# Four blocks of the output product's first token tile placed among the last pair's heads, with one PSUM layout for attention and output product

## The chip, the cores and the metric

The kernel runs on one core of a Trainium2 chip. The metric is the device time of one execution in microseconds (us). Each version is executed several times, and the median counts. The core's engines are TensorE (PE, whose weight loads are listed apart as PEld), VectorE (DVE), ScalarE (ACT), GpSimd (POOL) and SyncE (SP, which here issues nearly all DMAs). Each works through a queue of its own, in order; semaphores tie the queues together.

## What is computed

A trunk of two layers over 1024 tokens of width 1024, in fp32. Layer 0 has attention, layer 1 a recurrent block, and each is followed by a dense SwiGLU network. Only the end of attention and the output product behind it are touched here:

```python
def attention_mixer(h, w_in, rel_bias, w_out):
    ...
    out_a = chunked_relpos_attention(qa, ka, va, rel_bias)
    out_b = stick_breaking_attention(qs, ks, vs)
    return jnp.concatenate([out_a, out_b], axis=-1) @ w_out

def reference(x, ...):
    for layer in range(DEPTH):
        h = rmsnorm(x, norm_mix_pre[layer])
        m = attention_mixer(...) if layer % 2 == 0 else recurrent_mixer(...)
        x = x + rmsnorm(m, norm_mix_post[layer])
        h = rmsnorm(x, norm_ffn_pre[layer])
        x = x + rmsnorm(swiglu(h, ...), norm_ffn_post[layer])
    return x
```

There are 8 heads of the chunked softmax kind (`out_a`) and 8 of the stick-breaking kind (`out_b`), each 64 wide.

## The kernel before

**Heads in pairs.** `attention` (line 265) treats the 16 heads as 8 pairs of 128 columns; `p < 4` are softmax pairs, `p >= 4` stick-breaking ones. The order of pairs is `seq` (line 439): 4, 5, 6, 7, 0, 1, 2, 3, so the last pair is p = 3. For each pair `project` (line 305) computes q, k in two halves of 512 tokens each (line 311; three matmuls per weight block in lines 166 to 168, since every fp32 operand is held as a high and a low part), and lines 315 to 329 empty these banks into SBUF with DVE and ACT. `v_tile` (line 275) computes the values for two pairs at a time.

**One pair.** `attend` (line 332) goes over 8 query tiles `i` of 128 tokens. For each of the two heads `h` it computes scores (lines 387 and 388, in one or two chunks of at most 512 keys), which DVE reads at once together with the bias and the row minimum (line 391). ACT takes the exponential (line 399), DVE the reciprocal (401), POOL scales (402). PE then transposes the weights, four blocks to a bank (line 420, tile `tr`); ACT or DVE copies the bank to SBUF (424, 426), and PE multiplies by the values (line 350, into tile `pso`, weights 64 columns wide). After four query tiles ACT copies the output bank (line 436) and SP stores it (line 437). In the last pair the value products follow each group of transposes at once; in the other pairs they are collected into long runs.

**PSUM.** The core has eight banks of 128 x 512 fp32. In attention, two belong to projections (`proj`), three to scores (`sc`), one to outputs (`o`) and two to transposes (`tr`). They come from two pools that end with attention. In the last pair the scores of head 1 use the two `proj` banks, since no projection is left (lines 380 to 384). After attention the pools `pt` (two banks for transposes) and `po0` (three tiles `mm` of two banks each) are opened in the same eight banks.

**Output product.** `out_product` (line 552) multiplies the heads' outputs, read back from DRAM, by the output weights. It takes three token tiles of 128 at a time (t0 = 0, then 3, then the last two). For each of eight blocks `kt` of 128 rows, in the order 4, 5, 6, 7, 0, 1, 2, 3, it loads weights and splits them into high and low (lines 595, 155, 156; eight buffers `w`, so four pairs), does the same with the activations (593, 579, 580), and runs 6 matmuls for each token tile (line 569, 128x512 each), 18 for a block. The first block's activations lie in a tile of their own, `first` (line 588). When all blocks are summed, each token tile is normalised, added to x and transposed for the next stage.

**Order of work.** A planner lays out each engine's queue when the kernel is built: it follows the order of the program as a priority and a simulated time, so work that is written later may go ahead of work that has to wait. `behind` (line 199) adds an edge for this planner: what is issued inside it comes after the named instruction in the same engine's queue. It is no wait on the chip.

Of the kernel before, what the change touches and what calls it, by code (L numbers as in the profile page):

```python
# [99 lines left out]
class Trunk:  # L100
# [163 lines left out]

    def attention(self, x_src, xT_src, w_v, w_qk, bias_t, o_dst, hT):
        nc, tc = self.nc, self.tc
        with ExitStack() as ctx:
            ap = ctx.enter_context(tc.tile_pool(name="att", bufs=1, reuse_waits="tile"))
            prp = ctx.enter_context(tc.tile_pool(name="attproj", bufs=1, space=PSUM, reuse_waits="tile"))
            pp = ctx.enter_context(tc.tile_pool(name="attp", bufs=1, space=PSUM, reuse_waits="tile"))  # L270

# [3 lines left out]
            def v_tile(grp, w, vt, t2):  # L275
                ps = prp.tile([P, 512], F32, tag="proj", bufs=2, name=self.uid("psv"))
# [28 lines left out]
            def project(p, ws=(None, None)):  # L305
                st = [[ap.tile([P, S], F32R, tag="st", bufs=12, name=self.uid("st"))
                       for _ in range(3)] for _ in range(2)]
                for which in range(2):
                    w = ws[which] or self.split(w_qk[p, which], KT, P)
                    for half in range(2):  # L310
                        ps = prp.tile([P, 512], F32, tag="proj", bufs=2, name=self.uid("psq"))
                        self.proj_T(ps, w, slice(0, P), hT, half)
# [19 lines left out]
            def attend(p, st, vt):  # L332
# [26 lines left out]
                for i in range(NT):  # L359
# [3 lines left out]
                    if i % 4 == 0:  # L363
                        ops = pp.tile([P, 512], F32, tag="o", bufs=1, name=self.uid("pso"))
                    nat = []
                    n_c = 1 if n <= 512 else 2
                    w = n // n_c
                    for h in range(2):
# [10 lines left out]
                        for c in range(n_c):  # L379
                            if p == seq[-1] and h == 1:  # L380

                                sc = prp.tile([P, 512], F32, tag="proj", bufs=2, name=self.uid("sc"))[:, :w]
                            else:
                                sc = pp.tile([P, 512], F32, tag="sc", bufs=3, name=self.uid("sc"))[:, :w]
                            ks = slice(k0 * P + c * w, k0 * P + c * w + w)
                            cs = slice(c * w, c * w + w)
                            nc.tensor.matmul(sc, q, k1[:, ks], start=True, stop=False)
                            nc.tensor.matmul(sc, q, k2[:, ks], start=False, stop=True)
                            if p < 4:
                                off = 640 - n + c * w  # L390
                                nc.vector.tensor_tensor_reduce(
                                    pr[:, cs], sc, bias[h][:, off:off + w], 1.0, 3e38,
                                    op0=ALU.add, op1=ALU.min, accum_out=mn[c])
                            else:
                                nc.scalar.activation(pr[:, cs], sc, AF.Sigmoid, scale=rsc[:, i:i + 1])
# [7 lines left out]
                        else:  # L403
# [8 lines left out]
                            nc.gpsimd.memset(pr[:, n - 1:n], 0.0)  # L412
                        nat.append(pr)
                    blocks = [(kb, h) for kb in range(nb) for h in range(2)]
                    for b0 in range(0, len(blocks), 4):
                        bl = blocks[b0:b0 + 4]
                        tr = pp.tile([P, 512], F32, tag="tr", bufs=2, name=self.uid("tr"))
                        pt = ap.tile([P, 512], F32, tag="pt", bufs=7, name=self.uid("pt"))
# [19 lines left out]

            seq = [4, 5, 6, 7, 0, 1, 2, 3]
            vt = v_alloc()  # L440
            small = ap.tile([P, 64], F32, name="small")
# [25 lines left out]
            nc.vector.memset(ones, 1.0)  # L467
            warm = pp.tile([P, 512], F32, tag="tr", bufs=2, name=self.uid("warm"))
            for i in range(32):
# [23 lines left out]
            def spread(half):  # L493

                d = ap.tile([P, 1024], F32, tag="nat", bufs=4, name=self.uid("diag"))[:, :HALF]
                for i in range(4):
                    t = 4 * half + i
                    nc.vector.tensor_scalar(d[:, i * P:(i + 1) * P], self.ident, rsc[:, t:t + 1], None, op0=ALU.mult)
                ps = pp.tile([P, 512], F32, tag="tr", bufs=2, name=self.uid("psr"))
                nc.tensor.matmul(ps, ones, d, start=True, stop=True)  # L500
                nc.scalar.copy(rsb[:, half * HALF:(half + 1) * HALF], ps)
# [49 lines left out]

    def out_product(self, ap, pp, first, aT, w, x_src, x_dst, gpost_v, sink, kts):

# [8 lines left out]
        def psum():  # L562
            return pp.tile([P, D], F32, tag="mm", bufs=3, name=self.uid("ps"))
# [19 lines left out]
        for t0 in (0, 3):  # L583
            pst = [psum() for _ in range(3)]
            for kt in kts:
# [11 lines left out]
                split_act(a, ah, al)  # L597
                for t in range(3):
                    tok = slice(t * P, (t + 1) * P)
                    matmuls(pst[t], [(ah[:, tok], wh), (ah[:, tok], wl), (al[:, tok], wh)],  # L600
                            kt == kts[0], kt == kts[-1])
            if gpost is None:
# [487 lines left out]
    def run(self, out, stop=None):  # L1090
# [10 lines left out]
        ctx.enter_context(tc.tile_pool(name="edge", bufs=1, side="right")).tile([P, 48], F32, name="edge")  # L1101
        with pool("h0", "right") as hp:
            self.attention(x, io["x_t"], io["attn_w_v"], io["attn_w_qk"], io["bias_t"], oT, HiddenT(self, hp))

        def psum(name):
            return tc.tile_pool(name=name, bufs=1, space=PSUM, reuse_waits="tile")

        self.pt = ctx.enter_context(psum("pt"))

        early = []  # L1110
# [115 lines left out]
```

## Time and profile before

| | |
|---|---|
| median of 3 timed runs | 2199.62 us (2198.14 to 2202.62) |
| the profiled execution | 2196.73 us |
| its span, from first to last instruction | 2194.9 us |
| PE busy in the span | 2160.1 us, 98% |
| DVE, ACT, POOL busy | 70%, 53%, 10% |
| granted TensorE clock, mean | 0.998 |
| last pair's last value products | line 350, begun at 485.68 us |
| first matmul of the output product | line 569, at 486.58 us |

The page lists, for each engine, busy time and the number of instructions; views of the trace give instructions in order of time (start in us, duration, engine, line, operation, output<-inputs, shape; in brackets the idle time before it and what ended it), the waits by engine and line, and busy time by stretch of time. PE's matmuls are pipelined: one starts before the one ahead of it has ended, so the distance between starts says what a matmul takes of PE's time, not the duration printed. Times in the texts that look like 454.68 are microseconds from the start of the span.

### The profile page before, as it was taken

What the parts mean: (1) busy time and instruction counts of PE and PEld (TensorE: products, weight loads), DVE (VectorE), ACT (ScalarE), POOL (GpSimd) and SP (SyncE); (2) the same over time, 40 slices, a digit from 0 to 9 for tenths busy, and PEclk for the clock granted to TensorE, in tenths of its full rate; (3) what the DMA queues carried; (4) which work ended last, traced back from release to release, by engine and by line L of the source; (5) the groups of instructions that cost most, each with busy time, mean ns of one, the idle gap of its engine ahead of it and who ended that gap; (6) DMA issues with size and microseconds to landing.
All of it is one profiled execution on the core that took longest, in us unless ns stands there. A gap on an engine that the chain in (4) does not pass through costs nothing. (4 is left out here: it accounts for less than half of the span.)

```text
span 2194.9 us, 30583 instructions
## 1 busy us (share of the span) xinstructions
PE 2160.1 (98%) x11140; PEld 1800.3 (82%) x11140; DVE 1541.6 (70%) x2518; ACT 1171.8 (53%) x2174; POOL 217.2 (10%) x458
## 2 busy tenths in 40 slices
PE   9999999999999999999999999999999999999998
PEld 8888889878788888888887777888788888888886
DVE  5877765556878777776767677437787777758775
ACT  6655555556765444443436676527755444424443
POOL 1111113121100000000001333102000000000011
PEclk9999999999999999999999999999999999999999
DMA  7101011126423333236458411356233333328565
GB/s 274 34 30 49 21 44 49 54 92 211 140 92 111 117 100 115 92 124 228 146 175 258 132 61 39 96 193 218 93 120 111 103 114 97 110 87 287 172 182 155
DMA packets 168278, 270.21 MB, mean 123 GB/s; under 512 B 13888, under 2 KB 94784, under 8 KB 168128
## 3 DMA queue, kind: packets, MB, share of 16 engines
q1 hardware_dynamic: 167488, 266.18, 37.9%
q10 hardware_dynamic: 640, 2.10, 0.3%
q8 instruction: 87, 1.43, 0.3%
q14 instruction: 63, 0.52, 0.1%
HBM read 202.69 MB, written 65.54 MB: 122 GB/s over the span
## 5 line engine op out<-in xcount | busy, mean ns | idle before, releaser
L719 PE MATMUL ps<-hS,q 128*128 128x512 f32 (+1 forms) x1288 | 489.1, 380 | 0.9 <-DVE hS L89 0.9
L718 PE MATMUL ps<-hS,q 128*128 128x512 f32 (+1 forms) x1288 | 489.6, 381 | 0.3 <-ACT hS L96 0.3
L720 PE MATMUL ps<-hS,q 128*128 128x512 f32 (+1 forms) x1288 | 488.5, 380 | 0.0
L689 DVE TENSOR_TENSOR q<-raw,q 128x512 fp32r<-128x512 f32 x308 | 204.7, 685 | 173.3 <-ACT q L688 168.0
L719 PEld LDWEIGHTS ps<-hS,q 128*128 128x128 f32 x1288 | 242.2, 188 | 47.8 <-DVE hS L89 1.3
L718 PEld LDWEIGHTS ps<-hS,q 128*128 128x128 f32 x1288 | 241.7, 188 | 46.9 <-ACT hS L96 0.7
L720 PEld LDWEIGHTS ps<-hS,q 128*128 128x128 f32 x1288 | 242.2, 188 | 45.6
L688 ACT CAST q<-raw 128x512 fp32r<-128x512 f32 x308 | 178.6, 616 | 177.4 <-DVE raw L697 127.1
L804 PE MATMUL ps<-o,o 128*128 128x512 f32 x616 | 240.1, 390 | 0.2 <-DVE o L799 0.2
L805 PE MATMUL ps<-o,o 128*128 128x512 f32 x616 | 237.9, 390 | 0.5 <-DVE o L933 0.5
L803 PE MATMUL ps<-o,o 128*128 128x512 f32 x616 | 221.3, 391 | 2.5 <-ACT o L932 1.8
L676 ACT ACTIVATE raw<-raw,gcol 128x256 f32<-128x256 f32 x352 | 150.4, 498 | 130.2 <-DMA raw<-in_ffn_w_up_dram 69.6
L798 ACT CAST o<-raw 128x512 fp32r<-128x512 f32 x184 | 110.5, 620 | 158.0 <-PE ps L805 52.4
L182 POOL TENSOR_SCALAR rs<-ss 128x1 f32<-128x1 f32 x52 | 25.0, 481 | 1428.4 <-ACT junk L178 1362.7
L799 DVE TENSOR_TENSOR o<-raw,o 128x512 fp32r<-128x512 f32 x184 | 123.3, 687 | 54.0 <-ACT o L798 53.2
L803 PEld LDWEIGHTS ps<-o,o 128*128 128x128 f32 x616 | 115.5, 188 | 28.9 <-ACT o L932 3.7
L804 PEld LDWEIGHTS ps<-o,o 128*128 128x128 f32 x616 | 115.6, 188 | 25.2 <-DVE o L799 1.3
L805 PEld LDWEIGHTS ps<-o,o 128*128 128x128 f32 x616 | 115.6, 188 | 25.1 <-DVE o L933 1.3
L156 DVE TENSOR_TENSOR wlo<-raw,whi 128x1024 fp32r<-128x1024 f32 x76 | 93.5, 1230 | 57.5 <-ACT whi L155 56.3
L407 DVE TENSOR_TENSOR_SCAN pr<-pr,zero 128x128 f32<-128x128 f32 (+7 forms) x64 | 86.8, 1359 | 31.2 <-POOL pr L404 30.9
L155 ACT CAST whi<-raw 128x1024 fp32r<-128x1024 f32 x76 | 79.7, 1050 | 48.4 <-PE ps L167 20.2
L166 PE MATMUL psq<-hT,whi 128*128 128x512 f32 x256 | 102.0, 398 | 0.1
(205 smaller groups left out, 4308.4 us busy)
## 6 DMA issues: line engine op xcount, KB each, us to landing
raw<-in_ffn_w_gate_dram SPq DMA_DIRECT2D x44, 512.0 KB, 4.2
raw<-in_ffn_w_up_dram SPq DMA_DIRECT2D x44, 512.0 KB, 4.2
gS<-c SPq DMA_DIRECT2D x88, 256.0 KB, 3.7
raw<-gS SPq DMA_DIRECT2D x88, 256.0 KB, 2.8
gA<-c SPq DMA_DIRECT2D x66, 256.0 KB, 3.3
raw<-in_ffn_w_down_dram SPq DMA_DIRECT2D x63, 256.0 KB, 4.4
raw<-gA SPq DMA_DIRECT2D x44, 256.0 KB, 2.7
t<-in_ffn_w_down_dram SPq DMA_DIRECT2D x22, 512.0 KB, 6.8
```

Of the source, the lines that this page charges most:

```text
L166: nc.tensor.matmul(ps, wh[:, kt, cols], hh[:, kt, :], start=kt == 0, stop=False)
L676: nc.scalar.activation(raw[:, i], raw[:, i], AF.Copy, scale=gain[:, 4 * k + i:4 * k + i + 1])
L688: self.last = nc.scalar.copy(t[:, 0], src).ins
L689: self.last_lo = nc.vector.tensor_tensor(t[:, 1], src, t[:, 0].bitcast(F32), op=ALU.subtract).ins
L718: nc.tensor.matmul(ps, a[:, 0, kt, :], bh, start=kt == 0, stop=False)
L719: nc.tensor.matmul(ps, a[:, 0, kt, :], bl, start=False, stop=False)
L720: self.matmul = nc.tensor.matmul(ps, a[:, 1, kt, :], bh, start=False, stop=kt == 3).ins
L798: nc.scalar.copy(t[:, 0], src)
L799: tt(t[:, 1], src, t[:, 0].bitcast(F32), op=ALU.subtract)
L803: nc.tensor.matmul(ps, a[0], b[:, 0], start=first, stop=False)
L804: nc.tensor.matmul(ps, a[0], b[:, 1], start=False, stop=False)
L805: nc.tensor.matmul(ps, a[1], b[:, 0], start=False, stop=last)
```

## The change

PSUM is laid out once. The pool `pt` and the pool `po0` are opened before attention, and attention takes the three two-bank tiles of `po0` and cuts them into six banks: the first two for projections, the next three for scores, the last for outputs. They go round in the order of the program (`bank`). Head 1 of the last pair has no banks of its own any more; both heads use the three score banks. Transposes use the two banks of `pt`. The output product then takes the same three tiles again: token tile 0 gets the former projection banks, tile 1 two score banks, tile 2 the third score bank and the output bank.

In the last pair the last score matmul of each query tile is recorded in `self.scored`. In the output product of layer 0 (`ahead=True`; that of layer 1 is called as before) the first four blocks are prepared first, and their matmuls are issued together: token tile 0 of blocks 4, 5, 6, 7, and block number i of these only behind `scored[i + 1]`, the last score of query tile i + 1; then token tiles 1 and 2, block by block. The sums of a token tile are taken in the same order as before.

```diff
-    def attention(self, x_src, xT_src, w_v, w_qk, bias_t, o_dst, hT):
+    def attention(self, pp, x_src, xT_src, w_v, w_qk, bias_t, o_dst, hT):
...
-            prp = ctx.enter_context(tc.tile_pool(name="attproj", bufs=1, space=PSUM, reuse_waits="tile"))
-            pp = ctx.enter_context(tc.tile_pool(name="attp", bufs=1, space=PSUM, reuse_waits="tile"))
+            banks = [pp.tile([P, D], F32, tag="mm", bufs=3, name=self.uid("bank")) for _ in range(3)]
+            banks = [b[:, h * HALF:(h + 1) * HALF] for b in banks for h in range(2)]
+            turn = {"proj": banks[0:2], "sc": banks[2:5], "o": banks[5:6]}
+
+            def bank(tag):
+                turn[tag] = turn[tag][1:] + turn[tag][:1]
+                return turn[tag][-1]
+
+            def turned_bank():
+                return self.pt.tile([P, 512], F32, tag="tr", bufs=2, name=self.uid("tr"))
...
-                        ps = prp.tile([P, 512], F32, tag="proj", bufs=2, name=self.uid("psq"))
+                        ps = bank("proj")
...
-                        ops = pp.tile([P, 512], F32, tag="o", bufs=1, name=self.uid("pso"))
+                        ops = bank("o")
...
-                            if p == seq[-1] and h == 1:
-
-                                sc = prp.tile([P, 512], F32, tag="proj", bufs=2, name=self.uid("sc"))[:, :w]
-                            else:
-                                sc = pp.tile([P, 512], F32, tag="sc", bufs=3, name=self.uid("sc"))[:, :w]
+                            sc = bank("sc")[:, :w]
...
-                            nc.tensor.matmul(sc, q, k2[:, ks], start=False, stop=True)
+                            scored = nc.tensor.matmul(sc, q, k2[:, ks], start=False, stop=True).ins
...
+                    if p == seq[-1]:
+                        self.scored.append(scored)
...
-                        tr = pp.tile([P, 512], F32, tag="tr", bufs=2, name=self.uid("tr"))
+                        tr = turned_bank()
...
-            pst = [psum() for _ in range(3)]
+            pst, ready = [psum() for _ in range(3)], []
...
-                for t in range(3):
+                ready.append((kt, ah, al, wh, wl))
+                if ahead and t0 == 0 and len(ready) < 4 and kt in kts[:4]:
+                    continue
+                tiles = [(t, r) for r in ready for t in range(3)]
+                if len(ready) > 1:
+                    tiles.sort(key=lambda x: x[0] > 0)
+                for i, (t, (k, ah, al, wh, wl)) in enumerate(tiles):
                     tok = slice(t * P, (t + 1) * P)
-                    matmuls(pst[t], [(ah[:, tok], wh), (ah[:, tok], wl), (al[:, tok], wh)],
-                            kt == kts[0], kt == kts[-1])
+                    with self.behind([self.scored[i + 1]] if len(ready) > 1 and t == 0 else ()):
+                        matmuls(pst[t], [(ah[:, tok], wh), (ah[:, tok], wl), (al[:, tok], wh)],
+                                k == kts[0], k == kts[-1])
+                ready = []
...
-        with pool("h0", "right") as hp:
-            self.attention(x, io["x_t"], io["attn_w_v"], io["attn_w_qk"], io["bias_t"], oT, HiddenT(self, hp))
-
...
         self.pt = ctx.enter_context(psum("pt"))
+        first_banks = ctx.enter_context(ExitStack())
+        pp = first_banks.enter_context(psum("po0"))
+        with pool("h0", "right") as hp:
+            self.attention(pp, x, io["x_t"], io["attn_w_v"], io["attn_w_qk"], io["bias_t"], oT, HiddenT(self, hp))
...
-            with pool("o0", "right") as ap, psum("po0") as pp:
+            with pool("o0", "right") as ap, first_banks:
                 self.out_product(ap, pp, lambda *a: first(0, *a), oT,
                                  io["attn_w_out"], x, xs[0], io["norm_mix_post"][0],
-                                 hS, [4, 5, 6, 7, 0, 1, 2, 3])
+                                 hS, [4, 5, 6, 7, 0, 1, 2, 3], True)
```

More of the change, by code (lines that the diff above doesn't have):

```diff
@@ L275, in v_tile @@
             def v_tile(grp, w, vt, t2):
-                ps = prp.tile([P, 512], F32, tag="proj", bufs=2, name=self.uid("psv"))
+                ps = bank("proj")
                 for tt in range(2):
@@ L310, in project @@
                     for half in range(2):
-                        ps = prp.tile([P, 512], F32, tag="proj", bufs=2, name=self.uid("psq"))
+                        ps = bank("proj")
                         self.proj_T(ps, w, slice(0, P), hT, half)
@@ L439, in attention @@
             seq = [4, 5, 6, 7, 0, 1, 2, 3]
+            self.scored = []
             vt = v_alloc()
@@ L467, in attention @@
             nc.vector.memset(ones, 1.0)
-            warm = pp.tile([P, 512], F32, tag="tr", bufs=2, name=self.uid("warm"))
+            warm = turned_bank()
             for i in range(32):
@@ L498, in spread @@
                     nc.vector.tensor_scalar(d[:, i * P:(i + 1) * P], self.ident, rsc[:, t:t + 1], None, op0=ALU.mult)
-                ps = pp.tile([P, 512], F32, tag="tr", bufs=2, name=self.uid("psr"))
+                ps = turned_bank()
                 nc.tensor.matmul(ps, ones, d, start=True, stop=True)
@@ L550, in psum_t, with out_product @@
         return self.pt.tile([P, 512], F32, tag="tr", bufs=2, name=self.uid("pst"))
-    def out_product(self, ap, pp, first, aT, w, x_src, x_dst, gpost_v, sink, kts):
+    def out_product(self, ap, pp, first, aT, w, x_src, x_dst, gpost_v, sink, kts, ahead=False):
         nc = self.nc
```

## The prediction

> **What bounds the kernel now.** I read the page first, then a table by stretch of time, then TensorE's waits, then the order of instructions on PE and DVE around the end of attention.
>
> ```profile
> span 2194.9 us, 30583 instructions
> PE 2160.1 (98%) x11140; PEld 1800.3 (82%) x11140; DVE 1541.6 (70%) x2518; ACT 1171.8 (53%) x2174; POOL 217.2 (10%) x458
> ```
>
> PE counts as busy for 2160.1 of 2194.9 us; no other engine comes near. So the time is PE's work plus 34.8 us in which PE stands still, and a change that only moves work can win nothing but standing time. The table by stretch of time (start:end, length, then busy us and instruction counts of PE, PEld, DVE, ACT, POOL, then granted clock, DMA share, GB/s) shows how much of it lies where the change acts.
>
> ```profile
> 446.00:454.90 8.90, 6.92 (x71) 5.84 (x69) 8.59 (x25) 7.41 (x15) 1.06 (x2) 1.00 0.83 273
> 454.90:486.58 31.68, 29.83 (x279) 22.55 (x278) 19.40 (x84) 20.22 (x52) 12.85 (x19) 1.00 0.12 45
> 464.00:486.58 22.58, 22.58 (x220) 16.74 (x215) 12.33 (x55) 13.62 (x32) 8.25 (x11) 1.00 0.07 25
> 0.00:486.58 486.58, 473.96 (x3540) 414.36 (x3540) 330.83 (x651) 287.93 (x596) 92.77 (x238) 1.00 0.21 71
> 486.58:582.00 95.42, 95.42 (x419) 74.02 (x417) 64.08 (x90) 63.46 (x106) 13.99 (x26) 1.00 0.58 189
> ```
>
> The last pair (p = 3) runs its heads from about 452 to 486.58; there the output product starts. Between 454.9 and 486.58 PE lacks 31.68 - 29.83 = 1.85 us, all of it before 464. From 464 to 582 it lacks nothing. The rows of PE (start, duration, engine, line, operation, idle before) say which waits the 1.85 us are, and where the borders lie:
>
> ```profile
> 453.93 0.39 PE L387 MATMUL sc<-st,st 128*128 128x256 f32 x1 [1.15 <-DVE st L327]
> 454.68 0.28 PE L388 MATMUL sc<-st,st 128*128 128x256 f32 x1
> 455.38 0.39 PE L387 MATMUL sc<-st,st 128*128 128x512 f32 x1
> 455.85 0.34 PE L387 MATMUL sc<-st,st 128*128 128x384 f32 x1
> 456.20 0.82 PE L420 MATMUL tr<-ident,pr 128*128 128x128 f32 x6
> 458.36 0.44 PE L420 MATMUL tr<-ident,pr 128*128 128x128 f32 x2 [0.90 <-DVE pt L426]
> 459.54 0.63 PE L420 MATMUL tr<-ident,pr 128*128 128x128 f32 x4 [0.74 <-ACT pt L424]
> 461.94 0.41 PE L420 MATMUL tr<-ident,pr 128*128 128x128 f32 x2 [0.21 <-DVE pt L426]
> 475.73 0.30 PE L388 MATMUL sc<-st,st 128*128 128x320 f32 x1
> 486.58 0.50 PE L569 MATMUL ps<-whi,first 128*128 128x512 f32 x1
> 490.82 0.39 PE L569 MATMUL ps<-whi,ah 128*128 128x512 f32 x1
> 504.87 0.39 PE L569 MATMUL ps<-whi,al 128*128 128x512 f32 x1
> ```
>
> The waits are 0.90, 0.74 and 0.21 us, each a transpose waiting for DVE or ACT to empty a bank: 1.85 together. The score at 454.68 is the second 256-wide one, query tile 1 of head 1, which the change records as the second entry of its list; nothing moved may go ahead of it, so the 1.15 us before 453.93 stay out of reach.
>
> **The change part by part.**
>
> *What is moved.* Token tile 0 times four blocks is 4 x 6 = 24 matmuls of line 569 with their 24 weight loads. From 490.82 to 504.87 stand 62 steps (rows of first and last above), 14.05 / 62 = 0.227 us each, so 24 x 0.227 = 5.44 us of PE work leave the place behind 486.58. Nothing else is issued anew or moved by the edit: no DMA, so SP's and POOL's queues keep theirs, and no work of ACT or DVE. The operands stand ready in time already:
>
> ```profile
> 446.98 1.23 DVE L156 TENSOR_TENSOR wlo<-raw,whi 128x1024 fp32r<-128x1024 f32 x1 [0.15 <-ACT whi L155]
> 452.10 0.54 DVE L580 TENSOR_TENSOR al<-act,ah 128x384 fp32r<-128x384 f32 x1
> 490.79 1.05 ACT L155 CAST whi<-raw 128x1024 fp32r<-128x1024 f32 x1 [3.50 <-PE ps L569]
> 491.88 1.23 DVE L156 TENSOR_TENSOR wlo<-raw,whi 128x1024 fp32r<-128x1024 f32 x1 [6.29 <-ACT whi L155]
> 494.87 0.52 ACT L579 CAST ah<-act 128x384 fp32r<-128x384 f32 x1 [3.02 <-PE ps L569]
> 495.42 0.56 DVE L580 TENSOR_TENSOR al<-act,ah 128x384 fp32r<-128x384 f32 x1 [2.31 <-ACT ah L579]
> 486.70 0.59 ACT L436 COPY ob<-pso 128x512 f32<-128x512 f32 x1 [0.54 <-PE pso L350]
> ```
>
> The last low half of the four activations is made by 452.64. The fifth weight split can only begin at 490.79, when line 569 has freed the first pair of the eight "w" buffers; so the other four pairs were split before. The price of the move for the other engines is therefore nothing as long as these splits stay where they are; if the planner put them into the heads' time, four times 1.23 + 0.54 = 7.1 us of DVE would come in before 464, where DVE is busy 8.59 of 8.90 us at first.
>
> *What it fills.* If PE has such a matmul at hand in each of the three waits, 1.85 us go. The first two blocks (2.72 us) suffice. The rest of the 24 only change places with other PE work: 5.44 us more before, 5.44 us less behind.
>
> *What it adds between transposes.* A 512-wide matmul behind a run of transposes takes longer than one behind its like:
>
> ```profile
> 428.69 0.39 PE L168 MATMUL psq<-hT,wlo 128*128 128x512 f32 x1
> 428.92 0.39 PE L166 MATMUL psq<-hT,whi 128*128 128x512 f32 x1
> 429.15 0.38 PE L420 MATMUL tr<-ident,pr 128*128 128x128 f32 x2
> 429.29 0.48 PE L167 MATMUL psq<-hT,whi 128*128 128x512 f32 x1
> 429.60 0.31 PE L387 MATMUL sc<-st,st 128*128 128x320 f32 x1
> ```
>
> 428.69 to 428.92 is 0.23, 429.29 to 429.60 is 0.31: 0.08 us for each entry. Ends: nothing, where a block fills a wait; 24 x 0.08 = 1.9 us, if every matmul stood alone. I take four entries, 0.3 us, since the row nearest to it (the projection among the heads, six and more of a kind in a row) shows them mostly in runs.
>
> *The blocks without an edge.* Tiles 1 and 2 of the four blocks carry no edge. Tile 1 can start when the last score bank is read, just after 475.73, so it may land in the end of the heads, where transposes and value products take turns:
>
> ```profile
> 480.68 0.44 PE L350 MATMUL pso<-pt,v 128*64 128x128 f32 x4
> 481.05 0.66 PE L420 MATMUL tr<-ident,pr 128*128 128x128 f32 x4
> 481.64 0.66 PE L350 MATMUL pso<-pt,v 128*64 128x128 f32 x8
> 482.23 0.44 PE L420 MATMUL tr<-ident,pr 128*128 128x128 f32 x2
> ```
>
> Four value products take 0.37 us and eight take 0.59, so one is 0.055 and every visit costs 0.15 beside; for transposes the same sum gives 0.105 and about 0.16. PE counts as busy in this, so the 1.85 us are not all that PE loses, but a moved block does not remove a visit. An entry in that place costs 0.08 again: nothing to nine entries, 0.7; I take 0.3. The Trainium skill's page "TensorEngine Tiling (Array Packing)", section "Key Properties", says that a change of tiling mode drains TensorE. The 0.15 us beside the 64-column value products agree with it; by that rule a block set between value products of one group would pay two more such visits, four blocks 4 x 2 x 0.15 = 1.2 us, and the sum below would be -0.05 in place of -1.25 (the second rival has this case).
>
> *One PSUM layout.* In attention the banks now go round in program order: two for projection, three for scores, one for outputs, as many as before, except in the last pair: its head 1 had the two projection banks, and now both heads share three. Cost by both ends. Below nothing: the head-1 score no longer waits for a projection bank to be emptied, at most the 1.15 us of 453.93. Above: if the planner kept its order, the fourth of the five scores that stand at 453.93 to 455.85 would wait for DVE's read of the first:
>
> ```profile
> 456.43 0.41 DVE L391 CUSTOM_DVE_ANT_0 pr<-sc,bias 128x256 f32<-128x256 f32 x1
> 458.93 0.42 DVE L391 CUSTOM_DVE_ANT_0 pr<-sc,bias 128x256 f32<-128x256 f32 x1
> ```
>
> that is until 456.84 in place of 455.38, and the fifth until 459.35 in place of 455.85, 3.5 us, with the six transposes of 456.20 queued behind them on PE, and ACT and DVE waiting for those. I take nothing: the order is planned anew with three banks, and scores may come late without harm, since the last one (475.73) stands 10.9 us before 486.58, and PE works without a gap in between. Other pairs keep their numbers of banks; what a new plan does there I bound by the largest group of PE's waits in attention, whose four waits are 1.7 us at most: one more or one less.
>
> ```profile
> PE tr L420 <- DVE pr L410: 4.8, 4, 1.7
> ```
>
> *What is late next.* Behind the heads stand now 12 matmuls (2.72 us) for each of the first four blocks, so the fifth block is due 10.9 us after the heads, not 16.3. Its weights: first pair freed after 2.72, then 1.05 + 1.23 us of split, its activations after 5.4 + 0.52 + 0.56: ready at about 6.5. No new wait. Tile 2 needs the output bank copied by ACT (0.59 us) after the last value product; the 1.36 us of tile 1 hide it. From 486.58 to 582 PE has no gap today and the same work, so what is won arrives at the end.
>
> *Sum*: -1.85 + 0.3 + 0.3 + 0 = -1.25 us. The profiled execution took 2196.73 us, 1.83 over its span, and lies below all three timed runs (2198.14 to 2202.62); it becomes 2195.5. On the median of 2199.62 the same step gives 2198.4.
>
> **Rivals.**
>
> *A score waits at the head of PE's queue (slower).* One mechanism: with three banks the fourth score of a burst waits for a DVE read, and PE, in order, holds transposes and moved blocks behind it. It decides from the point where the planner puts four scores ahead of DVE's first read, as five stand at 453.93 to 455.85 now. Price 3.5 us, less the 1.85 us of waits that it swallows, plus the 0.6 of entries: +2.25, 2201.9. For it: DVE is the late engine until 457 (8.59 of 8.90). Against: the other pairs keep PE full with three. The Trainium skill's page "Perfetto Trace Analysis", section "Optimizing Tensor Performance", wants independent groups to rotate through different banks so that emptying one overlaps the next, which speaks for this rival. Chance 0.14.
>
> *Nothing is filled.* The planner sees no gap where the trace has one, or it splits groups of value products, whose extra visits (1.2 us) and the 0.6 of entries eat the gain of 1.85: 2199.6. For it: PE counts 22.58 of 22.58 us from 464. Against: 0.90 and 0.74 us are real waits right behind the permitted point. Chance 0.15.
>
> *More than the fill.* The new plan also loses the 1.15 us before 453.93, and one wait of 1.7 elsewhere: -1.25 - 2.85 = -4.1, 2195.5. Chance 0.13.
>
> *Halves tied together.* If two banks cut from one tile were ordered as one, projections would wait for each other's emptying: the 1.15 us of 453.93 for 32 projections, 37 us, 2236. Against it stands the later stage, which cuts its products from halves of one tile: ACT empties one while PE writes the other.
>
> ```profile
> 586.54 0.36 PE L718 MATMUL ps<-hS,q 128*128 128x256 f32 x1
> 586.54 0.36 ACT L724 COPY first<-ps 128x256 f32<-128x256 f32 x1
> ```
>
> Chance 0.03.
>
> **How the numbers follow.** The forecast, 2198.4, keeps 0.55. A measurement of this kernel can tell about 0.2%, 4.4 us, from no change: faster means below 2195.2, slower above 2204.0. Forecast, no fill and most of the first rival lie between. Below go half of the third rival and a little of the forecast's own spread of runs, 0.09; above go the tied halves and a share of the first rival, 0.07; 0.84 is left within. The range runs from 2194.6 (the third rival, less 0.9) to 2202.3 (the first rival, plus 0.4), which leaves out what lies outside by more than the runs' own spread.
>
> **What would show it.** Right: rows of the first tile's matmuls (line 569 now) stand on PE between about 455 and 470 where the 0.90 and 0.74 us were; PE's wait for DVE's and ACT's copies there falls from 1.85 to under 0.5; the stretch from the first transposes of the last pair to the first matmul of the fifth block is 1 to 2 us shorter; nothing changes on ACT, DVE and SP. Wrong: scores waiting for DVE's read on PE (first rival), the 24 matmuls behind the last value product (second), new waits at projections (fourth). A plan that differs far from the last pair, in order or in waits, would make the sum wrong in either direction.

## The result, and the profile after

| | before | after |
|---|---|---|
| median | 2199.58 us (2198.14 to 2202.62, 4 runs) | 2410.55 us (2404.39 to 2416.69, 4 runs) |
| ratio, 95% interval | | 1.0953 (1.0935 to 1.097) |
| profiled execution | 2196.73 us | 2404.39 us |
| mean granted clock | 0.998 | 0.966 |

The change costs 211 us, far outside the range. The page of the changed kernel begins:

```profile
span 2402.6 us, 30597 instructions
PE 2251.0 (94%) x11140; PEld 1843.6 (77%) x11140; DVE 1540.7 (64%) x2518; ACT 1175.2 (49%) x2174; POOL 225.1 (9%) x458
...
PEclk9789889999899999999999999999999999999999
```

The number of PE's instructions is the same, and DVE and ACT are as busy as before (1541.6 and 1171.8 us). PE stands for 2402.6 - 2251.0 = 151.6 us, before 34.8; it also counts as busy for 90.9 us more with the same matmuls, and five of the first eleven digits of the clock's row (granted clock by fortieths of the span, in tenths) are 7 or 8, where the kernel before has 9 throughout. The table by stretch of time says where (columns as in the prediction; the changed kernel first, then the kernel before). The cut at 692 us is not quite the end of the heads, whose last value products start at 701.02 with output matmuls already among them; it is where PE has done nearly as many matmuls as the kernel before by 486.58 (3532 and 3540).

```profile
0.00:692.00 692.00, 566.23 (x3532) 459.84 (x3532) 329.53 (x640) 291.07 (x590) 99.14 (x236) 0.89 0.14 50
692.00:2402.60 1710.60, 1684.74 (x7610) 1383.77 (x7608) 1211.16 (x1878) 884.16 (x1584) 125.98 (x222) 1.00 0.44 138
```

```profile
486.58:2194.90 1708.32, 1686.12 (x7602) 1385.99 (x7600) 1210.76 (x1867) 883.86 (x1578) 124.41 (x220) 1.00 0.44 138
```

From the cut on, both kernels take the same time within 2.3 us. The stretch ahead of it, attention, whose work the change only gave other banks, went from 486.58 to 692 us: 205.4 us, of which 113.2 are standing (125.8 against 12.6) and 92.3 more busy time, at a granted clock of 0.89. PE's waits in attention (engine, tile and line that waits, then the engine, tile and line waited for: total us, times, longest):

```profile
PE bank L392 <- ACT pr L400: 22.1, 29, 1.9
PE tr L427 <- DVE pr L415: 20.5, 15, 3.4
PE bank L392 <- DVE mn L396: 16.4, 21, 1.9
PE tr L427 <- POOL pr L407: 13.1, 15, 2.9
PE bank L166 <- DVE st L330: 11.0, 5, 4.3
...
PE bank L392 <- ACT ob L443: 4.4, 8, 0.8
```

Scores (line 392) now wait for the readers of score banks (lines 396 and 400), projections (166) for DVE's reading of a projection bank (330), and scores for ACT's copy of the *output* bank (443). The kernel before has none of these among its waits. The last one is the telling one: a score and the output copy have nothing in common but the two-bank tile. Rows of the changed kernel, two places:

```profile
211.22 0.69 DVE L330 SCALAR_TENSOR_TENSOR st<-bank,st 64x512 fp32r<-64x512 f32 x1
211.97 0.80 PE L166 MATMUL bank<-hT,whi 128*128 128x512 f32 x1 [1.25 <-DVE st L330]
...
222.51 0.68 ACT L400 ACTIVATE pr<-bank,small 128x512 f32<-128x512 f32 x1
223.24 0.50 PE L392 MATMUL bank<-st,st 128*128 128x512 f32 x1 [1.21 <-ACT pr L400]
```

Each PE row starts some 0.05 us after the reader above it has ended (211.91, 223.19). Which bank that reader read, the rows don't say: they leave out buffer numbers. The waits written in the changed program do (bank number + first column of the tile):

```
L166 writes bank5 + 512   waits for  DVE L330 reading bank5 + 0
L392 writes bank6 + 512   waits for  ACT L400 reading bank6 + 0
L392 writes bank7 + 0     waits for  ACT L443 reading bank7 + 512   (output copy)
```

So the program orders a write into one half of a two-bank tile behind the readers of the other half, though the halves are different banks. With two projection banks cut from one tile, PE cannot fill one while DVE empties the other.

### The profile page after: what moved, and what is told of

It reads as the page before. It is cut to its first block, busy times and chain, and to the rows that moved or that the text cites. A ratio compares the mean times of both kernels' runs of the same rounds, so it can differ in the third digit from the quotient of the medians.

```text
span 2402.6 us, 30597 instructions
## 1 busy us (share of the span) xinstructions
PE 2251.0 (94%) x11140; PEld 1843.6 (77%) x11140; DVE 1540.7 (64%) x2518; ACT 1175.2 (49%) x2174; POOL 225.1 (9%) x458
## 5 line engine op out<-in xcount | busy, mean ns | idle before, releaser
L427 PE MATMUL tr<-ident,pr 128*128 128x128 f32 x528 | 100.8, 316 | 42.5 <-DVE pr L415 20.5
L166 PE MATMUL bank<-hT,whi 128*128 128x512 f32 x256 | 114.3, 446 | 15.0 <-DVE st L330 11.0
```

What stands on the lines that cost most here:

```text
L166: nc.tensor.matmul(ps, wh[:, kt, cols], hh[:, kt, :], start=kt == 0, stop=False)
```

## The experiments

Theory: **the tie of two halves of one tile** is the whole loss. Rivals: the fixed turn of the banks, the blocks ahead, three score banks for the last pair's two heads, or tiles shared with the output product. Medians in brackets are those of the kernel before on the same chip.

**The layout alone.** The change without its blocks ahead.

```diff
-                                 hS, [4, 5, 6, 7, 0, 1, 2, 3], True)
+                                 hS, [4, 5, 6, 7, 0, 1, 2, 3])
```

> The changed PSUM layout alone: two-bank tiles cut into halves and turned in program order, but no block of the output product taken ahead. Theory (halves tied): a write to one half of a two-bank tile waits for the readers of the other half, all through attention; then the whole loss is here, 2400 to 2420 us. Rival (blocks): the 24 matmuls taken ahead and what they wait for make the loss; then 2196 to 2206.

Measured: 2414.32 us (2200.79), ratio 1.0967 (1.0925 to 1.1008). The loss is the layout's, not the blocks'.

**The same turn, a tile for each bank.** In attention's own pool:

```diff
...
-            banks = [pp.tile([P, D], F32, tag="mm", bufs=3, name=self.uid("bank")) for _ in range(3)]
-            banks = [b[:, h * HALF:(h + 1) * HALF] for b in banks for h in range(2)]
...
+            banks = [prp.tile([P, HALF], F32, tag="b%d" % i, bufs=1, name=self.uid("bank")) for i in range(6)]
...
```

> The same fixed turn of banks in program order (2 for projection, 3 for scores, 1 for outputs, the last pair's head 1 on the score banks too), but each bank a tile of its own, no block ahead. Theory (halves tied): the loss is gone, 2195 to 2206 us, and PE's waits for ACT's and DVE's reads of scores fall from about 39 us to under 3. Rival (fixed turn): banks that go round in the order of the program hold the scores up as before; then 2390 to 2420.

Measured: 2203.09 us (2200.79), ratio 1.0011 (0.9996 to 1.0026). The fixed turn is innocent, and so are three score banks in the last pair: together they cost at most 0.26%. PE's waits over the whole span show it: what was 16.4 us for line 396 is one wait.

```profile
PE tr L427 <- DVE pr L415: 4.8, 4, 1.7
...
PE bank L392 <- DVE mn L396: 1.6, 1, 1.6
```

**One tie at a time.** The last kernel again, but first only the projection banks are halves of one tile, then only the scores' and output banks, then the third score bank and the output bank alone, then all three pairs, still in attention's own pool (the lines of the first of the four):

```diff
...
+            pair = prp.tile([P, D], F32, tag="pair", bufs=1, name=self.uid("bank"))
+            banks = [pair[:, h * HALF:(h + 1) * HALF] for h in range(2)]
+            banks += [prp.tile([P, HALF], F32, tag="b%d" % i, bufs=1, name=self.uid("bank")) for i in range(4)]
...
```

> As e2_single_turn, but the two projection banks are halves of one tile again; scores and outputs have tiles of one bank. Theory (halves tied): a part of the loss comes back. In the changed kernel the waits of projection and value matmuls for emptied banks are 11.0 + 3.4 + 2.0 + 2.0 + 0.6 = 19 us of some 113 us that PE stands still in attention; so 2220 to 2260 us. Rival (fixed turn): as e2_single_turn, whatever that is.

> As e2_single_turn, but scores and outputs lie in halves of two tiles again (two score banks in one, the third with the output bank in the other); the projection banks are tiles of their own. Theory (halves tied): the larger part of the loss, 2330 to 2390 us, and together with the loss of e7_proj_tied about 211 us; PE's waits of scores for ACT's copy of the output bank are there again. Rival (fixed turn): as e2_single_turn.

> Only the output bank and the third score bank are halves of one tile. Outputs are copied once in four query tiles, so the tie should be met less often than that of two score banks: tie theory 2215 to 2270 us, with waits of scores for ACT's copy of the output bank (line 445) and of value products for DVE's or ACT's reading of scores. If the two score banks' own tie is the smaller part of the 158 us, this comes out above 2290. If ties cost nothing, 2203 as in the kernel with a tile for every bank.

> All three pairs of banks are halves of a two-bank tile, but in attention's own pools that end with it; the output product is as before. If the tie inside a tile is the whole loss, this gives the changed kernel's time, 2400 to 2420 us, and not the sum of the two single ties (2201 + 158 + 158 = 2517), since a write that waits for one neighbour finds the other's reader done. If sharing the tiles with the output product costs something of its own beside the ties, it stays well under: 2360 to 2395.

| tied | median (before) | ratio, 95% | clock |
|---|---|---|---|
| projections | 2358.54 (2200.79) | 1.0713 (1.0679 to 1.0747) | 0.974 |
| scores and output | 2358.79 (2200.79) | 1.0714 (1.0683 to 1.0745) | 0.971 |
| third score and output | 2342.70 (2198.99) | 1.0655 (1.0621 to 1.0688) | 0.971 |
| all three pairs | 2423.75 (2198.99) | 1.1023 (1.096 to 1.1086) | 0.960 |

All ties together, with nothing shared, cost about what the change costs: the intervals overlap, so the sharing adds nothing that these runs show. Each of the other three takes most of it already, so the losses overlap; that the first two would add up to about 211 us was wrong. Two expectations were too low: 2220 to 2260 for projections, 2215 to 2270 for the output bank; the 2400 to 2420 for all three pairs were missed by 4 us. The tie of the first two score banks was not run by itself. The waits of the kernels with tied projections and with the tied output bank:

```profile
PE bank L166 <- DVE st L332: 31.2, 12, 4.3
PE tr L429 <- DVE pr L417: 11.5, 13, 2.4
```

```profile
PE tr L429 <- DVE pr L417: 29.9, 12, 4.5
PE bank L394 <- DVE mn L398: 14.9, 17, 2.7
...
PE bank L394 <- ACT ob L445: 6.2, 8, 1.2
```

In the second, scores wait for the output copy itself for only 6.2 us in 8 waits; the larger loss is transposes (429) that wait for the attention weights, which DVE finishes in line 417 for the stick-breaking heads (29.9 us; 4.8 in the kernel with a tile for each bank). The rows of PE and ACT around one output copy show how the one becomes the other:

```profile
287.77 3.20 PE L429 MATMUL tr<-ident,pr 128*128 128x128 f32 x14 [4.36 <-DVE pr L417]
...
291.44 1.75 PE L361 MATMUL bank<-pt,v 128*64 128x128 f32 x28 [0.46 <-ACT pt L433]
293.11 0.50 PE L394 MATMUL bank<-st,st 128*128 128x512 f32 x1
...
302.55 4.06 PE L429 MATMUL tr<-ident,pr 128*128 128x128 f32 x16 [3.08 <-DVE pr L417]
...
306.83 2.76 PE L361 MATMUL bank<-pt,v 128*64 128x128 f32 x32 [0.22 <-ACT pt L433]
309.64 0.58 ACT L445 COPY ob<-bank 128x512 f32<-128x512 f32 x1 [2.59 <-PE bank L361]
310.28 0.38 PE L394 MATMUL bank<-st,st 128*128 128x256 f32 x1 [0.69 <-ACT ob L445]
```

Transposes, value products, scores, then standing until the weights from those scores are ready, transposes again, value products, the output copy, and only then the next score. The output bank collects four query tiles, and a score bank tied to it is not filled ahead of the value products that write the other half. The order of PE's queue in the two programs says the same: 64 scores use the third score bank; with the tie none of them stands ahead of a value product that the kernel writes earlier, with a tile of its own 56 do. So PE, DVE and ACT take turns where the scores used to run ahead. In all, PE stands 2344.0 - 2229.7 = 114.3 us here, 79.5 more than before. How much of the loss is the planned order and how much the waits on the chip, no run separates; both come from the tie.

**The blocks ahead without ties.** First two parts by themselves: three score banks in the last pair and else the kernel before; and the pools as before with the blocks asked for ahead.

```diff
-                            if p == seq[-1] and h == 1:
-
-                                sc = prp.tile([P, 512], F32, tag="proj", bufs=2, name=self.uid("sc"))[:, :w]
-                            else:
-                                sc = pp.tile([P, 512], F32, tag="sc", bufs=3, name=self.uid("sc"))[:, :w]
+                            sc = pp.tile([P, 512], F32, tag="sc", bufs=3, name=self.uid("sc"))[:, :w]
```

> The kernel before with one edit: the last pair's head 1 uses the three score banks in place of the two projection banks. The prediction took nothing for it, with ends -1.15 and +3.5 us; its first rival said +3.5 where nothing is moved ahead. Theory: within 1 us of before.

> The pools as before (attention's end with attention, those of the output product are opened behind them on the same banks, transposes' banks shared), the blocks asked for ahead as in the change. In the planned order none of the 24 matmuls stands ahead of the last value product, so this shows what the change would be without its one layout. Theory (ties): 2196 to 2204 us. Rival (the order t = 0 first for four blocks delays the fifth block): 3 us or more over before.

Measured: 2201.27 (2200.07), ratio 1.0007 (0.9998 to 1.0016); and 2200.79, ratio 1.0004 (0.9994 to 1.0013). No difference in either. In the second the output product's first matmul stands at 489.1 us, behind the heads: though asked for ahead, the blocks did not go ahead here, where their banks belong to pools that open after attention.

Then one layout for attention and output product in one-bank tiles that the planner hands out, so that the output product's norm has to read each token tile in two halves; with and without the blocks behind the recorded scores (the kernel's last two arguments, `ahead` and `shared`):

```diff
+            def bank(tag):
+                return pp.tile([P, HALF], F32, tag=tag, bufs={"proj": 2, "sc": 3, "o": 1}[tag], name=self.uid("bank"))
...
-            return self.post_norm_of([(slice(0, D), ps)], mg, x_src, x_dst, t, gpost, sink, ap, x)
+            return self.post_norm_of([(slice(0, 512), ps[0]), (slice(512, D), ps[1])], mg, x_src, x_dst, t, gpost, sink, ap, x, True)
...
-                                 hS, [4, 5, 6, 7, 0, 1, 2, 3], False, True)
+                                 hS, [4, 5, 6, 7, 0, 1, 2, 3], True, True)
```

> As e10_pairs_ahead, but no block goes ahead: the price of the layout in one-bank tiles and of the halved norm alone. Theory (ties): 2198 to 2204 us, no more than 2 us over before. Rival (one layout for both stages costs by itself): over 2210.

> The change without two-bank tiles: one PSUM layout for attention and output product in tiles of one bank each (2 projection, 3 score, 1 output, taken as they come free), a token tile of the output product takes two of them and its norm reads them in two halves; the four blocks go ahead among the last pair's heads. Theory (the ties alone made the loss, and the blocks fill waits): within 2 us of e11_pairs_plain, 1.25 us below it by the prediction's sum, and about 2196 to 2203 us; PE's standing time in the last pair 1 to 2 us less. Rival (the blocks themselves hold the heads up): 3 us or more above e11_pairs_plain.

Measured: without 2205.99 (2200.07), ratio 1.0030 (1.0019 to 1.0041); with the blocks 2210.25, ratio 1.0050 (1.0036 to 1.0063). Both lie above what the theory expected, 2198 to 2204 and 2196 to 2203, and the second is 4.3 us above the first, as the rival had it. Two things changed at once against the kernel before, so the halved norm was run by itself:

```diff
...
-            return self.post_norm_of([(slice(0, D), ps)], mg, x_src, x_dst, t, gpost, sink, ap, x)
+            return self.post_norm_of([(slice(0, 512), ps[:, 0:512]), (slice(512, D), ps[:, 512:D])], mg, x_src, x_dst, t, gpost, sink, ap, x, True)
```

> The kernel before, only that both output products' norms read each token tile as two halves of 512, the squares first, as the kernels with one-bank tiles must. PSUM and the order of attention are as before. If the halved norm is what the one-layout kernel without blocks ahead loses (2206.0 against 2200.1, a ratio of 1.0030), this is 2204 to 2207, ratio 1.002 to 1.004, with more standing of PE between 520 and 600 us and at the second product's norm near 1560 us. If that kernel's loss comes from its plan (output product among the heads) instead, this is within 0.1% of before: 2198 to 2202.

Measured: 2217.0 (2199.03), ratio 1.0083 (1.0069 to 1.0097): 18 us, more than either side expected. PE's transposes of the normalised rows now wait 14.8 us (the group's busy time, mean, idle time before it), in the kernel before 5.6, all for line 212:

```profile
L222 PE MATMUL pst<-ident,mg 128*128 128x128 f32 x128 | 18.6, 290 | 14.8 <-ACT mg L212 10.6 <-ACT mg L85 4.2
```

That is 9.2 of the 18 us; where the rest arises the runs don't say. With the same halved norms the layout in one-bank tiles took 2205.99 (1.0030): it had gained something, and the norm had hidden it. The next kernels take the norm in one piece in the second output product, with and without blocks ahead; then also for the first product's later token tiles, from banks laid out anew, again with and without:

```diff
+            ms = [(slice(0, D), ps[2])] if len(ps) == 3 else [(slice(0, 512), ps[0]), (slice(512, D), ps[1])]
...
+            if t0 and shared:
+                pp, shared = shared(), None
```

> The one layout with a tile for every bank and no block asked for ahead (2205.99, ratio 1.0030), but the second output product, which has its own banks, takes its norm in one piece again. The halved norm alone cost 18.0 us in two places (2217.0 against 2199.0). If the two places share it evenly, this is 9 us less: 2197, ratio 0.9985 to 0.9995. If the one layout itself gains nothing and the two losses only overlapped, it stays at 1.001 to 1.003.

> The same with the four blocks asked for ahead behind the recorded scores (with halved norms in both products 2210.25). 9 us less: 2201, ratio 1.000 to 1.001. It stays 3 to 5 us over the kernel without blocks ahead if the edges' order costs what it did there (a score waits 2.03 us for DVE at the head of PE's queue, and the clock falls).

> One layout in one-bank tiles for attention and the first three token tiles of the output product only, whose norm is halved; for the other five token tiles the banks are laid out anew in two-bank tiles, with the norm in one piece, as in the second product. No block is asked for ahead. If the halved norm was the whole loss and the early start of the output product a gain of 8 to 11 us, this beats the kernel before: 2190 to 2196, ratio 0.995 to 0.998. If the halved norm's loss sits in the first three tiles, it is as the kernel with the second product whole, 2196 to 2199.

> The same as the last with the four blocks asked for ahead: the change as it was meant, without tied halves and with the halved norm only where its tiles need it. If the predicted fill of 1.85 us is real, it is 1 to 2 us under the kernel without blocks ahead; if the planner's own choice is as good or better, 0 to 5 us over it.

| one-bank layout, norm in one piece | planner's own choice | blocks behind recorded scores |
|---|---|---|
| nowhere | 2205.99, 1.0030 | 2210.25, 1.0050 |
| second product (2198.44) | 2198.12, 0.9996 (0.9988 to 1.0005) | 2201.68, 1.0011 (1.0002 to 1.0020) |
| all but the first three token tiles (2198.44) | 2201.38, 1.0016 (1.0007 to 1.0025) | 2206.23, 1.0033 (1.0021 to 1.0046) |

The third row's kernel without the edges has fewer halved norms and was expected at 2190 to 2199, but it is slower than the second row's. It has one long wait that the second row's kernel has not, at 522.71 us, where the output product waits for the norm to read the old banks before they are laid out anew:

```profile
PE ps L580 <- DVE mg L250: 4.1, 1, 4.1
```

In each row the blocks behind recorded scores are slower than the planner's own choice, by 4.3, 3.6 and 4.9 us. Note what this compares: in these layouts the planner sets matmuls of the output product among the heads unasked, so neither column is a kernel without early matmuls. The stretch around the waits of 1.85 us shows a part of the difference; first the kernel before, then the kernel of the second row without the edges, then with them:

```profile
440.00:490.00 50.00, 46.17 (x425) 36.66 (x425) 30.54 (x118) 30.76 (x74) 14.71 (x21) 1.00 0.26 92
```

```profile
440.00:490.00 50.00, 48.82 (x411) 40.55 (x410) 30.10 (x116) 29.14 (x69) 14.76 (x21) 1.00 0.25 87
450.00:460.00 10.00, 10.00 (x83) 8.91 (x80) 7.89 (x27) 5.90 (x16) 3.35 (x5) 1.00 0.71 263
```

```profile
440.00:490.00 50.00, 46.88 (x391) 39.28 (x391) 30.77 (x119) 30.28 (x71) 15.48 (x22) 0.97 0.25 87
450.00:460.00 10.00, 7.57 (x62) 6.53 (x63) 8.43 (x33) 6.99 (x19) 2.60 (x4) 0.83 0.79 281
```

Left to itself the planner puts the output product's first matmul ahead of all that, and fills the whole stretch from 450 to 460:

```profile
448.99 0.50 PE L580 MATMUL ps<-whi,first 128*128 128x512 f32 x1 [0.91 <-ACT first L591]
```

With the edges they may not come before the second query tile's last score. Ahead of that, a score of the first query tile (128 wide) stands at the head of PE's queue, waiting for DVE, and the first block comes only at 457.31, behind it and the second tile's two scores:

```profile
455.83 0.33 PE L387 MATMUL bank<-st,st 128*128 128x128 f32 x1 [1.64 <-DVE mn L391]
```

From 440 to 490 PE thus stands for 50 - 46.88 = 3.12 us with the edges, 1.18 without them, and 3.83 in the kernel before. The lower clock is not the whole of it: in the third row's kernel with the blocks the clock was 1.00 from 450 to 460, and the edges cost it no less.

What the filled stretch is worth is read from the start of the next stage, its first matmul, in the first of the two times behind the three durations (min/median/max ns); the kernel before, the halved norm alone, the planner's own choice, and the blocks behind scores:

```profile
L718 PE MATMUL ps<-hS,q x1288: 278/389/681, 581.7 to 1975.5; 128*128 128x512 f32 x168, 128*128 128x256 f32 x16
```

```profile
L718 PE MATMUL ps<-hS,q x1288: 278/389/679, 585.8 to 1992.3; 128*128 128x512 f32 x168, 128*128 128x256 f32 x16
```

```profile
L738 PE MATMUL ps<-hS,q x1288: 278/389/682, 579.8 to 1976.5; 128*128 128x512 f32 x168, 128*128 128x256 f32 x16
```

```profile
L738 PE MATMUL ps<-hS,q x1288: 278/389/682, 585.1 to 1980.3; 128*128 128x512 f32 x168, 128*128 128x256 f32 x16
```

With the same halved norm in the first product, the one layout with the planner's early start is 585.8 - 579.8 = 6.0 us ahead, and the edges give 5.3 of it back (one profiled execution each). A last run asked whether the order of the halved norm's readers could be mended:

```diff
-            return self.post_norm_of(ms, mg, x_src, x_dst, t, gpost, sink, ap, x, True)
+            return self.post_norm_of(ms, mg, x_src, x_dst, t, gpost, sink, ap, x)
```

> As the one-layout kernel with the second product's norm whole (2198.12, ratio 0.9996), but in the halved norm of the first product DVE multiplies both halves by the gain before ACT squares them, so that the banks' readers run in another order. If the order of the two readers is what the halved norm loses, this beats the kernel before: 2190 to 2195, ratio below 0.998. If it is the number of instructions (two squares, two products, one more addition for each token tile), it is the same within 0.1%: 2196 to 2201.

Measured: 2199.96 (2200.44), ratio 0.9997 (0.9988 to 1.0006), as with the other order (0.9996): the order does not matter. No version beat the kernel before by more than its runs differ.

## Why the prediction was wrong

**The step that failed** is the term "One PSUM layout", "I take nothing", together with the dismissal of its last rival, "Halves tied together" (chance 0.03). That rival is what happened. It was set aside because "ACT empties one while PE writes the other" in a later stage. The rows at 586.54 show ACT reading a `ps` and PE writing a `ps`, and say nothing of which. In the program of the kernel before, the matmul at 586.54 belongs to another product, in another tile; the other half of the tile that ACT reads is written only by the product after it, and that one waits:

```
L718 writes ps1208 + 0     first product of the stage
L718 writes ps1212 + 0     at 586.54, another tile
L718 writes ps1208 + 512   waits for  ACT L724 reading ps1208 + 0
```

So the tie stood in the kernel before as well, in the very rows quoted against it, and cost nothing there because a product in another tile lay between.

**Its price** was too small too: 37 us against 211. It priced the projections alone, at one wait of 1.15 us each. The runs show three things missing. The projections' tie by itself costs 158 us, with waits of up to 4.3 us; the scores' and output banks are tied as well, 158 us by themselves; and the granted clock was lower with the standing (0.974 and 0.971 in these two kernels; the section on the hardware has a close view).

**The fill, -1.85 us**, cannot be read from the changed kernel, whose loss covers it. Without ties it came only in part. With the blocks behind the scores the waits of 0.90 and 0.74 us are gone (PE has no wait from 457.31 to 465 in the second row's kernel), but PE stands for 1.18 and 1.64 us ahead of them instead, so that from 440 to 490 it stands only 0.7 us less than in the kernel before. With the planner's own choice, which sets output matmuls before the score that waits 1.64 us, it stands 2.65 us less. Against this choice the edit's edges cost 3.6 to 4.9 us; the forecast, though, compared with a kernel that has no early matmul at all, and such a kernel was not run with the same layout and norms. The nearest pair has both norms halved: 2217.0 (1.0083) in the old layout with nothing early, 2210.25 (1.0050) in the one layout with the blocks. So these runs do not refute the sign of the fill. The prediction's limit, "nothing moved may go ahead of it, so the 1.15 us before 453.93 stay out of reach", was the edge's limit and not the chip's: without the edge the planner filled that place. The first rival, a score at the head of PE's queue, occurred in those kernels (1.64 and, with the halved norm in both products, 2.03 us; 3.5 were forecast), though the three banks alone cost nothing that could be measured (1.0007).

**What held**: the order of the blocks and the 24 early matmuls do stand among the last pair's heads in the changed kernel (the first at 637.69); no other engine has more work; and from the cut at 692 us on, time is unchanged within 2.3 us. The 0.3 us each for entries and for blocks without an edge cannot be read under a loss of this size, and stay open.

**Still open**: how the 18 us of the halved norm arise, since the order of its readers did not matter; why the edges cost 3.6 to 4.9 us where the standing they leave is 1.9; and how much of the 92 us of extra busy time in attention is clock. By an estimate from the window, as if busy time grew in step with the missing clock, it is 566.23 x (1 - 0.89) = 62 us; no run separates the rest.

## What to carry to other kernels

Give every PSUM bank that should turn independently a tile of its own: the programs of these kernels order a write into one half of a shared tile behind the readers of the other half, and one such tie cost 144 us (a score bank and the output bank, which collects four query tiles) or 158 us (the two projection banks). Do not take two adjoining rows of a trace for proof that two buffers are independent, since the names leave out which buffer it is; look for the wait in the program, or run the layout alone. To fill a gap, make the work possible before the gap begins and leave the place to the planner: an edge that ends inside the gap left PE standing for 3.12 us where the planner's own choice left 1.18.

## What the runs showed of the hardware

In attention the short waits came with a lower granted clock, 0.89 on average against 1.00 in the kernel before, and the loss was more than their own length: 92.3 us of busy time came on top of the 113.2 of standing. Three neighbouring windows of the changed kernel around 211.97:

```profile
205.00:212.00 7.00, 3.94 (x21) 2.32 (x19) 5.82 (x6) 4.80 (x10) 0.69 (x3) 0.87 0.00 0
212.00:217.00 5.00, 5.00 (x12) 3.95 (x13) 0.90 (x1) 0.00 (x0) 0.10 (x1) 0.50 0.00 0
217.00:222.00 5.00, 5.00 (x28) 4.05 (x26) 1.37 (x1) 2.40 (x4) 0.29 (x1) 1.00 0.00 0
```

PE stood 3.06 of 7 us, in four gaps of 0.24 to 1.25 us; then it ran 5 us at a clock of 0.50, 12 matmuls of 0.42 us each, where the prediction's rows have 0.227 for the same shape. The Trainium skill's page "TensorE: Matmul & The Clock Gate", section "HAM oscillation — how this bites in real kernels", gives as its rule that TensorE must not idle for longer than about 3.4 us, and has the clock fall to half behind a longer wait. The half clock agrees with the 0.50; the length does not, since here the fall followed gaps of at most 1.25 us that came close together. The Trainium skill's page "TensorE: Matmul & The Clock Gate", section "A second HAM failure mode: psum-queue depth-cycling", reports such a rise and fall from another kernel whose TensorE idled shortly but often between groups of matmuls, without a length. A fall is not certain: from 450 to 460 the kernel of the second row with the blocks behind scores (7.57 us busy) got 0.83, while the kernel before, no busier, kept 1.00:

```profile
450.00:460.00 10.00, 7.19 (x66) 5.78 (x60) 8.59 (x34) 6.82 (x20) 3.79 (x6) 1.00 0.71 258
```
